# Where the low part of each weight comes from: a subtraction on VectorE, or an accumulating transfer onto the negated rounded block

## The chip, the cores and the metric

The kernel runs on one core of a Trainium2 chip. The metric is device time in microseconds, from one launch of the whole program; the kernel before took 977.54 us as the median of three runs. One core has five engines that take part here: TensorE (PE, matrix products; PEld is its weight load), VectorE (DVE), ScalarE (ACT), GpSimd (POOL) and SyncE (SP, which here only issues transfers). Each engine works through its own queue of instructions in order, and they wait for each other by semaphores. Sixteen DMA engines move data between the chip's memory (HBM) and the on-chip memory (SBUF). Products land in PSUM, from where ScalarE and VectorE fetch them.

## The reference

One inference step of a one-layer hybrid model on 640 tokens (128 context tokens, 512 latent tokens on a grid of 8 x 64), width 1024. With `h` the normed and modulated input:

```python
h = rmsnorm(x, norm1_g) * (1 + sc1) + sh1            # sh, sc, g: six rows from silu(c) @ w_ada
q, k, v, o, gates, u, ga, gb = split(h @ w_in + b_in) # 1024 -> 512*4 + 16 + 1024 + 1024 + 1024
A = (sigmoid(o) * headnorm(mlstm_both_ways(q, k, v, gates))) @ w_proj_a
B = silu(layernorm(dwconv31(glu(u)))) @ w_proj_b
x = x + g1 * ((sigmoid(ga) * A + sigmoid(gb) * B) @ w_out)
h2 = rmsnorm(x, norm2_g) * (1 + sc2) + sh2
gate, val = split(h2 @ w_up)                          # 1024 -> 2 * 2816
x = x + g2 * ((gelu(dwconv3x3(gate)) * val) @ w_down) # 2816 -> 1024
y = rmsnorm(x, final_norm_g)
```

All of it is in float32. The context's final mLSTM states are outputs as well.

## The kernel before

**Products.** Features lie on the 128 partitions, tokens along the free dimension. TensorE works on float32r operands, a rounded form of float32, so every operand is split into a rounded high part and a low part that holds the rest. One 128 x 128 weight block times 128 features then takes three products: high by high, high weight by low input, low weight by high input (`three`, line 443). `mtile` (457) does this for all 640 tokens in two halves of 320, six products for each weight block. `mhalf` (1203) does it for one part of the tokens only, three products for each block. The half-width stages are the output projection (`woA`, `woB`, line 1294), the first columns of the up projection (`upA`, `upB`, 1397), and the second half of the down projection (`dnA` with 384 tokens, `dnB` with 256, line 1466).

**Weight stream.** `_blocks` (82) lists the 1160 weight blocks in the order of their use, eight to a group, 145 groups of 128 x 1024 float32 (512 KB). Three functions feed them:
- `load` (401) has SP load a group from HBM into a staging tile `wst`, of which there are three (NST).
- `prep` (408) splits a group: ScalarE copies `wst` to the rounded `wh`, and VectorE subtracts, `wl = wst - wh`. There are three tiles of `wh` and three of `wl` (NWT), so the tiles of group g + 3 take the place of those of group g.
- `W` (428) hands TensorE its block. On the first block of group g it calls `prep` for g, g + 1 and g + 2 and `load` for g + 3 and g + 4. HELD changes that where two groups are in use side by side: at the start, and in the two v stages (groups 9 and 10, 19 and 20), where no further split is made until both groups are done.

**Order.** The order of all instructions is written out by a planner. `_Order` (143) keeps an estimated clock for every engine; `issue` (203) moves it with each instruction. The main line is the large products. Side lines are generators (norms, gates, the mLSTM scans, the splits of `prep`), which go on when the planner thinks that their operands are there. Background work (convolution taps, the modulation products `ada_tile`, the taps of the feed-forward's convolution) fills VectorE where the planner sees it idle. Every instruction goes through the wrapper `_Timed`, so the profile gives the same line, L139, for all of them, and groups have to be told apart by tile names: `wst`, `wh`, `wl` are the weight stream; `hh`, `hl` the normed input; `h2h`, `h2l` the second one; `mgh`, `mgl` the merged branches; `ah`, `al`, `acth`, `actl` the activations of the feed-forward; `adst` and `ad` the modulation weights; `mm` and `ps` are in PSUM.

**GpSimd** does only memsets, of tiles for the gates (`keep`, `bc`, `dd`, `M`, in `gates`, 792), for the convolution's padding, and of `gbuf` for the feed-forward.

**Start.** x (16 transfers of x in all, eight here) and the first modulation weights (`adst`, 16 transfers of 512 KB) come in while the first products run: for each of the eight feature tiles, four column tiles (`FIRST`) take their products as soon as this tile of the normed input is there. Groups 0 to 3 belong to this stage.

Of the kernel before, what the change touches and what calls it, by code (L numbers as in the profile page):

```python
# [9 lines left out]
F32 = mybir.dt.float32  # L10
# [42 lines left out]
# f tiles in the order of the up projection, and which of them each half of the down projection sums  # L53
# [19 lines left out]
# column tiles whose products run while x and the first modulation come in, then the order of all tiles  # L73
# [8 lines left out]
def _blocks():  # L82
    """Order in which the 128 x 128 weight blocks are used: (matrix, k block, column block)."""
    b = []
    held = {0: 2, 1: 3}
    for k in range(KD):
        b += [(nm, k, m) for nm, m in FIRST]
    for nm, m in ORDER:
        if nm == "v":
            held[len(b) // GB] = len(b) // GB + NWT  # L90
            held[len(b) // GB + 1] = 0
            b += [("v", k, 2 * m + i) for k in range(KD) for i in range(2)]
        else:
            for mm in (m, m + 4) if nm == "u" else (m,):
                if (nm, mm) not in FIRST:
                    b += [(nm, k, mm) for k in range(KD)]
    for nm, m in BRANCH:
        if nm == "g":
            b += [(n, k, m) for n in ("ga", "gb") for k in range(KD)]
        else:  # L100
            b += [("p" + nm, k, m) for k in range(4)]
    b += [("woA", k, m) for m in range(2) for k in range(KD - 1)] + [("woA", KD - 1, m) for m in range(2)]
    b += [("woA", k, m) for m in range(2, 8) for k in range(KD)]
    b += [("woB", k, m) for m in range(8) for k in range(KD)]
    for nm in ("upA", "upB"):
        b += [(nm, k, m) for k in range(KD) for m in (0, NF)] + [(nm, k, 1) for k in range(KD)]
    b += [("up", k, NF + 1) for k in range(KD)]
    for i, (fs, ks) in enumerate(zip(UPS, DNS)):
        for f in fs[2:] if i == 0 else fs:
            b += [("up", k, f) for k in range(KD)]  # L110
            b += [("up", k, NF + f) for k in range(KD)]
        for nm, npre in (("dn", 0),) if i == 0 else (("dnA", 3), ("dnB", 0)):
            b += [(nm, f, m) for m in range(npre) for f in ks[:-1]]
            b += [(nm, ks[-1], m) for m in range(npre)]
            b += [(nm, f, m) for m in range(npre, 8) for f in ks]
    return b, held
# [8 lines left out]
class _Timed:  # L125
    """An engine whose instructions also move an estimate of when their results are there."""
# [17 lines left out]
class _Order:  # L144
    """Emits the instructions of several lines of work in one order: the main line (large products) sets the
    pace, side lines go on when what they last asked of other engines should be there, and background work
    fills VectorE where it would be idle."""
# [55 lines left out]
    def issue(self, key, name, ops, args, kw):  # L203
        out, ins = ops[0], ops[1:]
        acc = kw.get("accum_out")
        t = max([self.free.get(key, 0.0)] + [self.ready.get(a.tensor.name, 0.0) for a in ins if a is not acc])
        if key == "Q":
            t = max(t, self.now)
        t = max(t, self.avail.pop(out.tensor.name, 0.0))
        if key in ("V", "S", "G"):  # L210
            t = max(t, self.ready.get(out.tensor.name, 0.0) - self.LAT)
        t += self.cost(key, name, ops, args, kw) * (2 if key == "PE" and t < COLD else 1)
        self.free[key] = t
        done = t + (2000.0 if key == "Q" else self.LAT)
        for a in (out,) if acc is None else (out, acc):
            self.ready[a.tensor.name] = done
        for a in ops:
            self.used[a.tensor.name] = max(done, self.used.get(a.tensor.name, 0.0))
        if self.line is not None and key in ("V", "S", "G"):
            self.line[0] = max(self.line[0], done)  # L220

    def ring(self, key, tile_, bufs):
        """A tile that takes the place of the one handed out `bufs` tiles before it."""
        names = self.rings.setdefault(key, [])
        names.append(tile_.tensor.name)
        if len(names) > bufs:
            self.avail[names[-1]] = self.used.get(names[-1 - bufs], 0.0)
        return tile_

    def force(self, t):  # L230
        """Runs a side line to its end without regard to the clock."""
        while not t[2]:
            self._go(t)

    def before(self, ops):
        """Background work for the time VectorE would wait for these operands."""
        while self.idle_work() and not self.filling:
            t = max(self.ready.get(a.tensor.name, 0.0) for a in ops[1:] or ops)
            if t < self.free.get("V", 0.0) + HOLE:
                break  # L240
            self.fill()
# [18 lines left out]
    def until(self, *tiles):  # L260
        """Holds a side line until these tiles should be there."""
# [6 lines left out]
    def room(self, key):  # L268
        """Holds a side line while an engine has more than a little left to do."""
# [27 lines left out]
    def fill(self):  # L297
        """One piece of background work, from the lanes in turn: two in a row rarely wait for each other."""
# [19 lines left out]
def tile_trunk(  # L318
# [18 lines left out]
    V, S, G, PE, Q = (_Timed(e, od, k) for e, k in ((nc.vector, "V"), (nc.scalar, "S"), (nc.gpsimd, "G"),  # L337
                                                    (nc.tensor, "PE"), (nc.sync, "Q")))
# [69 lines left out]
    def prep(g):  # L408
        """Splits the eight blocks of group g into two float32r parts that add up to them exactly."""
# [7 lines left out]
        def parts():  # L417
            yield from od.until(src)
            S.activation(hi, src, AF.Copy)
            yield  # L420
            V.tensor_sub(lo, src, hi.bitcast(F32))
# [21 lines left out]
    def three(out, whl, xhl, first, last, shared=0):  # L443
        """out += (hi + lo of one operand) x (hi + lo of the other), without lo x lo. Where two products share the
        bank of their first output, they are one group: one opens it (shared = 1), the other closes it (2)."""
# [18 lines left out]
    def views(pt, t, rows=slice(0, P)):  # L464
        """Where a product lies in PSUM, and the part of a feature-major tile it belongs to."""
# [4 lines left out]
    def split(src, name, hi=None, lo=None):  # L470
        """float32 tile [P, T] -> its two float32r parts."""
# [29 lines left out]
    def rstd(src, w, scale, name):  # L501
        """(src * scale + EPS) ** -0.5, the table's square root refined by one Newton step."""
# [11 lines left out]
    def sqrt_table():  # L514
        """Has the square root's table loaded ahead of its use."""
# [62 lines left out]
    def ada1():  # L578
        """Shift and scale of the first norm, 128 features at a time, and the normed input they give."""
# [190 lines left out]
    def v_tile(p):  # L770
        """v by tokens, heads 2p and 2p + 1."""
# [129 lines left out]
    def setup(p):  # L901
        """Products q k, k by tokens, decay matrices and scaled q of heads 2p, 2p + 1."""
# [295 lines left out]
    def pieces(s):  # L1198
        """Context and latent tokens of a range: (condition, first, end)."""
# [21 lines left out]
    def norm_add(m, s, pc):  # L1221
        """Square of a range of x2[m] now, its column sums once TensorE has other work in between."""
# [4 lines left out]
    def norm_flush():  # L1227
        """Column sums of the squares that should be there."""
# [156 lines left out]
    def dn(fn, mat, m, fs, *args, **kw):  # L1385
        """Down products over f tiles, each taken when it is there."""
# [42 lines left out]
    def square_sum(m, s, sums):  # L1429
        """Adds the square of a range of x2[m] to the sum over the first tiles; the last stays by itself."""  # L1430
# [50 lines left out]
def _columns(v):  # L1481
    """(n * 128,) or (..., n * 128) -> [128, ... n]"""
# [128 lines left out]
```

## Time and profile before

| | before |
|---|---|
| time, median of three runs | 977.54 us (975.96 to 978.05) |
| profiled execution: span, first to last instruction | 976.2 us |
| TensorE busy | 952.3 us, 6796 products |
| VectorE busy | 730.5 us, 1336 instructions |
| ScalarE busy | 362.2 us, 658 instructions |
| GpSimd busy | 6.0 us, 41 instructions |
| moved by DMA | 113.01 MB |
| granted TensorE clock, mean | 0.994 |

The profiled execution has no other time shown than its span; the median of the runs lies 1.3 us above it.

How to read the lines: a line of a group gives line, engine, operation, output tile <- input tiles, shape, count, then busy time and mean ns of one, then the idle time of the engine before them and what ended it. A line of the chain of waits or of the timeline gives the start in us from the span's start, the duration, the engine and the operation. PEld is the weight load of TensorE. A line of a table by stretches gives, after the stretch and its length, the busy time of each engine with its count, then the granted clock, the share of time that the DMA engines were busy, and GB/s. A matmul's duration contains its way through the array; products follow each other about 146 ns apart, though each is shown with some 309 ns.

### The profile page before, as it was taken

What the parts mean: (1) busy time and instruction counts of PE and PEld (TensorE: products, weight loads), DVE (VectorE), ACT (ScalarE), POOL (GpSimd) and SP (SyncE); (2) the same over time, 40 slices, a digit from 0 to 9 for tenths busy, and PEclk for the clock granted to TensorE, in tenths of its full rate; (3) what the DMA queues carried; (4) which work ended last, traced back from release to release, by engine and by line L of the source; (5) the groups of instructions that cost most, each with busy time, mean ns of one, the idle gap of its engine ahead of it and who ended that gap; (6) DMA issues with size and microseconds to landing.
All of it is one profiled execution on the core that took longest, in us unless ns stands there. A gap on an engine that the chain in (4) does not pass through costs nothing.

```text
span 976.2 us, 16639 instructions
## 1 busy us (share of the span) xinstructions
PE 952.3 (98%) x6796; PEld 927.1 (95%) x6796; DVE 730.5 (75%) x1336; ACT 362.2 (37%) x658; POOL 6.0 (1%) x41
## 2 busy tenths in 40 slices
PE   5999999999999999999999999999999999999996
PEld 2799999999998999999999999999999999999995
DVE  3849989998887989898778877985323777675565
ACT  5453434345643422223675333232111232323342
POOL 0100000000000000000000000000000000000000
PEclk9999999999999999999999999999999999999998
DMA  9635122211242355667433222322222222223353
GB/s 355 238 108 87 44 73 66 69 45 55 84 134 76 108 194 183 206 222 274 138 123 117 72 92 76 130 86 66 83 70 65 87 69 84 65 87 95 122 172 109
DMA packets 38971, 113.01 MB, mean 116 GB/s; under 512 B 4336, under 2 KB 7280, under 8 KB 38896
## 3 DMA queue, kind: packets, MB, share of 16 engines
q1 hardware_dynamic: 38896, 111.96, 35.1%
q8 instruction: 53, 0.87, 0.3%
q14 instruction: 22, 0.18, 0.1%
HBM read 108.79 MB, written 3.15 MB: 115 GB/s over the span
## 4 chain that ended last, share of the span: by engine, by line
PE 95%; ACT 2%; DVE 1%; DMA 1%; issue 0%; SPq 0%; DVEq 0%; ACTq 0%
PE mm L139 87%; PE ps L139 8%; DMA x<-in_xT 1%; ACT wh L139 0%; ACT L139 0%; DVE rsy L139 0%; ACT h L139 0%; DVE yo L139 0%; ACT h2h L139 0%; DVE rst L139 0%; ACT sq L139 0%; SPq L139 0%; DVE wl L139 0%; ACT rsy L139 0%; ACT hh L139 0%
## 5 line engine op out<-in xcount | busy, mean ns | idle before, releaser
L139 ACT ACTIVATE wh<-wst 128x1024 fp32r<-128x1024 f32 x145 | 152.9, 1057 | 195.8 <-PE mm L139 175.4
L139 DVE TENSOR_TENSOR wl<-wst,wh 128x1024 fp32r<-128x1024 f32 x145 | 176.3, 1220 | 60.3 <-ACT wh L139 60.1
L139 PE MATMUL mm<-h2h,wh 128*128 128x320 f32 x704 | 164.4, 309 | 0.7 <-ACT h2h L139 0.7
L139 PE MATMUL mm<-h2l,wh 128*128 128x320 f32 x704 | 164.6, 309 | 0.4 <-DVE h2l L139 0.4
L139 PE MATMUL mm<-h2h,wl 128*128 128x320 f32 x704 | 164.0, 308 | 0.0
L139 PE MATMUL mm<-hh,wh 128*128 128x320 f32 (+2 forms) x576 | 134.6, 313 | 3.5 <-ACT wh L139 2.5
L139 PE MATMUL mm<-hl,wh 128*128 128x320 f32 (+2 forms) x576 | 133.4, 311 | 0.0
L139 PE MATMUL mm<-hh,wl 128*128 128x320 f32 (+2 forms) x576 | 133.4, 310 | 0.0
L139 DVE SCALAR_TENSOR_TENSOR acc<-gbuf,cols,acc 128x455 f32<-128x455 f32 (+2 forms) x176 | 129.7, 742 | 4.4
L139 PEld LDWEIGHTS mm<-h2l,wh 128*128 128x128 f32 x704 | 118.8, 188 | 1.1 <-DVE h2l L139 0.9
L139 PEld LDWEIGHTS mm<-h2h,wh 128*128 128x128 f32 x704 | 118.6, 188 | 1.3 <-ACT h2h L139 1.2
L139 PEld LDWEIGHTS mm<-h2h,wl 128*128 128x128 f32 x704 | 118.5, 188 | 0.0
L139 DVE SCALAR_TENSOR_TENSOR z<-glu,cols,z 128x641 f32<-128x641 f32 (+14 forms) x120 | 102.2, 888 | 0.8
L139 PEld LDWEIGHTS mm<-hh,wh 128*128 128x128 f32 x576 | 96.2, 188 | 5.8 <-ACT wh L139 3.0
L139 PEld LDWEIGHTS mm<-hl,wh 128*128 128x128 f32 x576 | 96.4, 188 | 2.1 <-issue 1.3
L139 PEld LDWEIGHTS mm<-hh,wl 128*128 128x128 f32 x576 | 96.8, 188 | 0.7 <-issue 0.7
L139 PE MATMUL mm<-ah,wl 128*128 128x320 f32 (+2 forms) x320 | 85.5, 308 | 0.0
L139 PE MATMUL mm<-ah,wh 128*128 128x320 f32 (+2 forms) x320 | 85.5, 308 | 0.0
L139 PE MATMUL mm<-al,wh 128*128 128x320 f32 (+2 forms) x320 | 85.5, 307 | 0.0
L139 DVE SCALAR_TENSOR_TENSOR junk<-ad,cb 128x512 bf16<-128x512 f32 x128 | 81.9, 686 | 0.0
L139 PEld LDWEIGHTS mm<-ah,wl 128*128 128x128 f32 x320 | 56.7, 188 | 0.1
L139 PEld LDWEIGHTS mm<-al,wh 128*128 128x128 f32 x320 | 56.8, 188 | 0.0
(224 smaller groups left out, 1288.7 us busy)
## 6 DMA issues: line engine op xcount, KB each, us to landing
wst<-in_w SPq DMA_DIRECT2D x145, 512.0 KB, 3.6
ad<-in_ada SPq DMA_DIRECT2D x64, 256.0 KB, 3.0
adst<-in_ada SPq DMA_DIRECT2D x16, 512.0 KB, 10.3
x<-in_xT SPq DMA_DIRECT2D x16, 320.0 KB, 5.7
out_yT<-x SPq DMA_DIRECT2D x8, 192.0 KB, 4.5
cb<-in_crow SPq DMA_DIRECT2D x4, 256.0 KB, 5.6
out_yT<-yo SPq DMA_DIRECT2D x4, 256.0 KB, 2.2
Ca<-in_cst SPq DMA_DIRECT2D x1, 516.0 KB, 6.9
```

The costliest lines, as they stand in the source:

```text
L139: return fn(*args, **kw)
```

## The change

The split of a group no longer has a subtraction. ScalarE writes the rounded copy `wh` as before, and then a second copy of `wst`, scaled by -1, into `wl`: the negated rounded block. Then GpSimd's queue issues a transfer of the same 512 KB from HBM with an accumulate, `wl += w`, which leaves `w - wh` in `wl`. Each weight group is thus read twice from HBM, once by SP into `wst` and once by the accumulating transfer. The planner gets a key "R" for this queue: a transfer starts no earlier than TensorE's estimated clock and the readiness of its output, and its result is there 2000 ns after its modelled cost.

The split's side line now issues its three instructions in one go; before, it gave way to others between the copy and the subtraction. The comments and docstrings of the file are gone too, which changes line numbers only.

```diff
@@ class _Order, issue
-        if key == "Q":
+        if key in ("Q", "R"):
             t = max(t, self.now)
+        if key == "R":
+            t = max(t, self.ready.get(out.tensor.name, 0.0))
...
-        done = t + (2000.0 if key == "Q" else self.LAT)
+        done = t + (2000.0 if key in ("Q", "R") else self.LAT)
@@ tile_trunk
-    V, S, G, PE, Q = (_Timed(e, od, k) for e, k in ((nc.vector, "V"), (nc.scalar, "S"), (nc.gpsimd, "G"),
-                                                    (nc.tensor, "PE"), (nc.sync, "Q")))
+    V, S, G, PE, Q, GQ = (_Timed(e, od, k) for e, k in ((nc.vector, "V"), (nc.scalar, "S"), (nc.gpsimd, "G"),
+                                                        (nc.tensor, "PE"), (nc.sync, "Q"), (nc.gpsimd, "R")))
@@ prep
         def parts():
             yield from od.until(src)
             S.activation(hi, src, AF.Copy)
-            yield
-            V.tensor_sub(lo, src, hi.bitcast(F32))
+            S.activation(lo, src, AF.Copy, scale=-1.0)
+            GQ.dma_start(lo, w_d[g], accum_op=ALU.add)
+            yield
```

## The prediction

> **What bounds the kernel now.** I read the page's busy shares and its chain of waits first, then who TensorE waits for, then single stretches of the timeline.
>
> ```profile
> span 976.2 us, 16639 instructions
> PE 952.3 (98%) x6796; PEld 927.1 (95%) x6796; DVE 730.5 (75%) x1336; ACT 362.2 (37%) x658; POOL 6.0 (1%) x41
> ...
> PE 95%; ACT 2%; DVE 1%; DMA 1%; issue 0%; SPq 0%; DVEq 0%; ACTq 0%
> ```
>
> ```profile
> PE ps L139 <- DVE rsy L139: 3.0, 3, 2.0
> PE mm L139 <- ACT wh L139: 2.5, 1, 2.5
> PE mm L139 <- DVE ga L139: 1.0, 1, 1.0
> ```
>
> TensorE (PE) is busy for 98% of the span and is 95% of the chain. The waits in which it waits for VectorE (DVE) come to about 4 us in all; none names the tile wl that the removed subtraction writes. So lightening VectorE can win some 4 us at best, and the question is whether the new way makes wl late.
>
> ```profile
> L139 ACT ACTIVATE wh<-wst 128x1024 fp32r<-128x1024 f32 x145 | 152.9, 1057 | 195.8 <-PE mm L139 175.4
> L139 DVE TENSOR_TENSOR wl<-wst,wh 128x1024 fp32r<-128x1024 f32 x145 | 176.3, 1220 | 60.3 <-ACT wh L139 60.1
> ...
> wst<-in_w SPq DMA_DIRECT2D x145, 512.0 KB, 3.6
> ...
> adst<-in_ada SPq DMA_DIRECT2D x16, 512.0 KB, 10.3
> ```
>
> ```profile
> q1 hardware_dynamic: 38896, 111.96, 35.1%
> ```
>
> Of the 195.8 us that ScalarE (ACT) idles before wh, 175.4 us end with TensorE. That is the three-buffer ring: wh and wl of group g+2 take the place of those of g-1, so a split can begin only when TensorE has left g-1, and has two group periods until it is used. The timeline of an output projection group shows the margin:
>
> ```profile
> 479.33 0.42 PE L139 MATMUL mm<-mgh,wh 128*128 128x320 f32 x1
> ...
> 480.13 1.05 ACT L139 ACTIVATE wh<-wst 128x1024 fp32r<-128x1024 f32 x1
> ...
> 481.20 1.23 DVE L139 TENSOR_TENSOR wl<-wst,wh 128x1024 fp32r<-128x1024 f32 x1 [1.09 <-ACT wh L139]
> ...
> 483.33 0.41 PE L139 MATMUL mm<-mgh,wh 128*128 128x320 f32 x1
> ...
> 487.31 0.42 PE L139 MATMUL mm<-mgh,wh 128*128 128x320 f32 x1
> ...
> 487.57 0.19 PEld L139 LDWEIGHTS mm<-mgh,wl 128*128 128x128 f32 x1
> ```
>
> Groups start at 479.33, 483.33 and 487.31: a period p of 3.99 us. The split starts 0.80 us after the group's start, wl is there at 482.43, and its first weight load is 0.26 us into the group two later, at 487.57: 5.1 us to spare.
>
> **The change part by part.** *Removed:* 145 subtractions, 145 x 1.220 = 176.9 us of VectorE. As TensorE hardly waits for VectorE, I take 0; bounds are 0 and the 4 us above. VectorE's background taps then run earlier, which TensorE does not wait for either.
>
> *Added on ScalarE:* 145 negated copies of the same shape as wh: 145 x 1.057 = 153 us, to 53% of the span. Each holds back evacuations of PSUM behind it by 1.06 us, covered by the second product buffer for one period. Where ScalarE itself is on the chain there is no cover:
>
> ```profile
> 503.87 1.06 ACT wh L139
> ...
> 509.04 1.04 ACT wh L139
> ...
> 512.09 1.05 ACT wh L139
> 513.14 0.02 issue
> 513.16 1.23 DVE wl L139
> ```
>
> Three copies are added there and one subtraction leaves: 3 x 1.05 - 1.23 = +1.9 us. With late weights in these six groups as well I take +4; bounds 2 and 15.
>
> *Added on DMA:* 145 accumulating transfers of 512 KB, issued from GpSimd's queue. The load by SP stays, so in_w is read twice, and each transfer also reads wl back. Let L be the time from the end of the negated copy to landing. No row shows an accumulate or a transfer issued by GpSimd. From below: 3.6 us, the plain load of the same bytes, of which this does everything and more. From above: 10.3 us, the same size in the crowded start. Between: queue q1 took 0.351 x 976.2 / 111.96 = 3.06 us per MB, 1.6 us for 0.524 MB; reading wl back should cost that again, 3.6 + 1.6 = 5.2, and about 1 us for descriptors in software, for which no row stands (0 to the 5.1 us left below 10.3). I take L = 6.2 where DMA is quiet and 7.8, one load of 1.6 us more, where it is crowded; nearer to 3.6 than to 10.3, since most of the program is not like the start.
>
> The Trainium skill (Collectives: The Full Stack, section "The bandwidth ceiling") says that an add in the DMA path costs not for the arithmetic but for its second source read, which halved the rate there (1.93). By that the accumulate's data would take twice a load's 1.6 us, as assumed; no trace here shows it yet.
>
> The allowed L follows from the timeline. From group start to the end of hi and negated copy: 0.80 + 2 x 1.06 + about 0.1 of semaphore = 3.02; use at 2p + 0.26. So **L must be under 2p - 2.8**, and beyond it each group costs (L - 2p + 2.8) / 2. Periods, by stage:
>
> ```profile
> 514.85 417.94 PE mm L139 x2795
> ```
>
> ```profile
> 894.62 1.06 ACT L139 ACTIVATE wh<-wst 128x1024 fp32r<-128x1024 f32 x1 [2.50 <-PE mm L139]
> 898.81 1.06 ACT L139 ACTIVATE wh<-wst 128x1024 fp32r<-128x1024 f32 x1 [3.13 <-PE mm L139]
> ```
>
> ```profile
> 0.00:40.00 40.00, 28.97 (x256) 17.74 (x257) 18.46 (x52) 19.33 (x34) 4.26 (x33) 0.96 0.91 352
> 441.00:465.00 24.00, 24.00 (x201) 22.00 (x199) 19.75 (x50) 9.71 (x14) 0.00 (x0) 1.00 0.71 250
> 465.00:503.00 38.00, 38.00 (x310) 35.66 (x310) 25.96 (x46) 24.42 (x44) 1.30 (x2) 1.00 0.41 134
> ...
> 934.80:964.90 30.10, 30.10 (x275) 29.80 (x274) 21.66 (x36) 12.76 (x18) 0.00 (x0) 1.00 0.49 158
> ```
>
> (After the busy times come granted clock, DMA share and GB/s.) A full group is 48 products of 149.5 ns, p = 7.2, so L may be 11.6: **no cost** for some 97 of 145 groups. The half-width groups pay:
> - Output projection, 16 groups, p = 3.99, allowed 5.2. Five are in the stretch with DMA at 0.71: (7.8 - 5.2) / 2 x 5 = 6.5; eleven at (6.2 - 5.2) / 2 = 5.5. Sum 12.
> - First part of the last down projection (384 tokens), 11 groups, p = 4.2 (894.62 to 898.81), allowed 5.6: 0.3 x 11 = 3.3.
> - Second part (256 tokens), 11 groups in 30.1 us, p = 2.74, allowed 2.7. **This is below even the plain load's 3.6.** With loads, accumulates and outputs together it is crowded: (7.8 - 2.7) / 2 x 11 = 28.
> - The two v stages hold two groups at once, so the next group is split one period ahead: allowed 7.2 - 2.8 = 4.4, (6.2 - 4.4) x 2 = 3.6.
> - The start:
>
> ```profile
> 22.17 1.04 ACT L139 ACTIVATE wh<-wst 128x1024 fp32r<-128x1024 f32 x1
> ...
> 23.63 1.22 DVE L139 TENSOR_TENSOR wl<-wst,wh 128x1024 fp32r<-128x1024 f32 x1
> ...
> 26.99 0.36 PEld L139 LDWEIGHTS mm<-hh,wl 128*128 128x128 f32 x2
> ```
>
> The copies end at about 24.3, wl is wanted at 26.99, and DMA is 0.91 busy: 24.3 + 7.8 - 27.0 = 5.1.
>
> *Queue of GpSimd.* Each transfer waits there for its negated copy; behind it stand the memsets and later transfers. The gate memsets now come after the first groups' transfers:
>
> ```profile
> 25.15 1.91 POOL L139 MEMSET keep<- 64x640 f32 x11 [8.73 <-PE ps L139]
> ```
>
> They would run some tens of us later, and with the gate scans held back; TensorE has the q, k and u tiles to do meanwhile, so 0, and about 4 us (these and three of 0.63) without that cover. SP's loads gain a little: a wst buffer comes free after the copy instead of the later subtraction.
>
> **Sum:** 5.1 + 3.6 + 12 + 4 + 3.3 + 28 = 56, so 976.2 + 56 = 1032 of span. The median of the runs (977.54) is 1.3 above this span, whose own execution has no other time shown: **1033 us.** With L = 3.6 everywhere: 0.9 + 0 + 0 + 2 + 0 + 5 = 8, or 985. With 10.3 everywhere: 7.6 + 11.8 + 41 + 15 + 26 + 42 = 143, or 1121.
>
> **Rivals.** *Not slower: VectorE's relief.* If the transfers land as fast as the subtraction did, within 2.7 us in the 256-token part, nothing stalls, and the waits on rsy and ga (4.0 us) plus the subtraction on the chain at 513.16 (1.2) go: 977.5 - 5 = 972. It speaks for it that 97 groups have 11.6 us; against it that the plain load alone takes 3.6, and that the 4 us are mostly reciprocals and not queueing. It decides at L = 2.7. If it lands at about 3, losses and gains meet: no change, 977.
>
> *Saturated DMA.* If an accumulate occupies the 16 engines for four times a load (6.4 us), group and load need 8.0 us against a period of 7.2, and the full groups bind too: 145 x 8.0 = 1160, plus the 37 MB of other transfers, partly under it: about 1200. It decides at 7.2 - 1.6 = 5.6 us per accumulate. For it: elementwise work in the DMA path is nowhere in this trace. Against: the share is 35%, and would be 35 + 145 x 3.2 / 976 = 83% by my estimate.
>
> *The clock falls with the stalls.* If gaps of 1 to 2.5 us in every half-width group lower the granted clock to half, their products take twice as long: output projection +64, second down part +30, against the 40 they cost by stalls: 1033 + 54 = 1087. Against it: in the first 40 us TensorE is idle for 11 us and the clock is 0.96. The Trainium skill (TensorE: Matmul & The Clock Gate, section "HAM oscillation") says that idle gaps beyond about 3.4 us put the clock back to half; by that rule gaps of my size would be too short, and the row of the start agrees as far as it goes.
>
> *Not what it says:* the subtraction is gone from the program text, and exactly one copy and one transfer stand in its place; I give this nothing.
>
> **How the numbers follow.** Late weights in the half-width stages, as summed: 0.70, own range 985 to 1080. Saturated DMA 0.12, clock 0.05, relief 0.06, no change 0.07. This kernel's measurement can tell about 0.2% (2 us) from no change. So faster 0.06, same 0.07, slower 0.87. The range takes in the bounds of L (985 to 1121), part of the no-change case below and part of the saturated case above: 978 to 1145.
>
> **What would show it.** wl should be written by ScalarE 145 times at 1.06 us and by a GpSimd transfer, with DMA at about 188 MB; VectorE near 554 us, ScalarE near 515. TensorE should wait for the DMA of wl in the output projection, from about 935 on and near 27 us, and not in full-width stretches. Median issue-to-landing of the accumulate should be 5 to 8 us. The forecast is wrong if that is under 4 us, or above 11, or if TensorE's new waits name something else than wl.

## The result and the profile after

The changed kernel takes 1080.51 us (median of four runs, 1079.84 to 1082.76) against 976.75 us of the kernel before (four runs, the three above among them): a ratio of 1.107, 95% interval 1.105 to 1.109, 104 us slower. The prediction of 1033 us had the direction, most of the places, and 56 of the 104 us. The time lies inside its range of 978 to 1145, at the upper edge of the 985 to 1080 that it gave to late weights by themselves.

The page of the kernel after, its busy shares, queues and issues (an issue line ends with the median us from issue to landing):

```profile
span 1078.1 us, 16901 instructions
...
PE 983.9 (91%) x6795; PEld 952.0 (88%) x6796; DVE 572.1 (53%) x1191; ACT 496.5 (46%) x803; POOL 131.9 (12%) x186
...
q0 software_dynamic: 20880, 76.03, 38.5%
q1 hardware_dynamic: 38896, 111.96, 33.4%
...
wst<-in_w SPq DMA_DIRECT2D x145, 512.0 KB, 4.1
wl<-in_w POOLq DMA_DIRECT2D x145, 512.0 KB, 7.6
ad<-in_ada SPq DMA_DIRECT2D x64, 256.0 KB, 5.6
```

Three things are to be seen. VectorE lost 158 us of work, as meant, and that bought nothing. The accumulate lands after 7.6 us, where a plain load took 3.6 before, and the other loads became slower beside it (wst 3.6 to 4.1, ad 3.0 to 5.6; the line of ad in the kernel before is the one below). And TensorE, with the same number of products, was idle for 94.2 us instead of 23.9, but was also *busy* for 31.6 us longer.

```profile
ad<-in_ada SPq DMA_DIRECT2D x64, 256.0 KB, 3.0
```

Whom TensorE's products wait for, longest first:

```profile
PE mm L139 <- DMA wl<-in_w: 62.1, 27, 6.0
PE ps L139 <- ACT sq L139: 8.4, 5, 4.3
PE mm L139 <- DVE ga L139: 8.2, 1, 8.2
```

The first row is new: 27 waits of up to 6.0 us for the low part. The third was 1.0 us. One of the 27, in the timeline of the output projection:

```profile
498.50 0.19 PEld L139 LDWEIGHTS mm<-mgh,wh 128*128 128x128 f32 x1
...
499.28 1.04 ACT L139 ACTIVATE wh<-wst 128x1024 fp32r<-128x1024 f32 x1
...
500.23 1.04 ACT L139 ACTIVATE wl<-wst 128x1024 fp32r<-128x1024 f32 x1
...
501.56 0.86 POOL L139 DMA_DIRECT2D wl<-in_w  x1 [10.53 <-ACT wl L139]
...
506.47 0.19 PEld L139 LDWEIGHTS mm<-mgh,wh 128*128 128x128 f32 x1
...
507.39 1.04 ACT L139 ACTIVATE wh<-wst 128x1024 fp32r<-128x1024 f32 x1
...
509.06 0.19 PEld L139 LDWEIGHTS mm<-mgh,wl 128*128 128x128 f32 x1 [2.29 <-DMA wl<-in_w]
```

A group starts at 498.50, the copies begin 0.78 us later and end at 501.27. The group two later starts at 506.47 and would want its low part at about 506.7; it comes at 509.06, 7.8 us after the copies. The copies for a later group begin at 507.39, while TensorE waits: they need the group before this one to be over, and not its low part.

Cut at the last product of the start and at the first products with the convolution's output, the merged branches and the feed-forward's activations, so that a stage holds the same products in both kernels, the table by stretches reads as follows (busy time and count of each engine, then granted clock, DMA share, GB/s), first for the kernel before, then for the kernel after:

```profile
0.00:63.10 63.10, 52.07 (x424) 40.07 (x424) 33.38 (x80) 28.80 (x48) 4.26 (x33) 0.97 0.73 271
63.10:334.00 270.90, 268.46 (x1963) 262.10 (x1962) 238.34 (x475) 123.99 (x277) 0.44 (x6) 1.00 0.26 73
334.00:432.10 98.10, 98.10 (x673) 98.10 (x672) 87.74 (x208) 23.87 (x28) 0.00 (x0) 1.00 0.55 182
432.10:495.00 62.90, 62.90 (x503) 59.02 (x502) 48.33 (x100) 32.93 (x54) 1.30 (x2) 1.00 0.62 213
495.00:668.60 173.60, 172.53 (x1182) 170.96 (x1182) 145.08 (x224) 66.08 (x121) 0.00 (x0) 1.00 0.29 96
668.60:886.10 217.50, 217.50 (x1485) 217.50 (x1485) 125.47 (x166) 55.39 (x90) 0.00 (x0) 1.00 0.24 76
886.10:965.00 78.90, 78.90 (x562) 77.86 (x561) 47.24 (x74) 30.43 (x40) 0.00 (x0) 1.00 0.42 134
```

```profile
0.00:77.20 77.20, 56.65 (x423) 43.85 (x424) 26.91 (x74) 34.37 (x54) 9.24 (x36) 0.89 0.81 262
77.20:365.40 288.20, 271.77 (x1962) 265.95 (x1962) 231.89 (x532) 153.60 (x309) 28.81 (x41) 0.98 0.61 144
365.40:478.60 113.20, 103.16 (x671) 102.37 (x671) 69.69 (x186) 35.83 (x41) 11.25 (x13) 0.96 0.82 233
478.60:564.30 85.70, 70.59 (x504) 64.04 (x502) 19.12 (x48) 48.34 (x71) 13.60 (x17) 0.92 0.85 192
564.30:746.00 181.70, 175.60 (x1181) 173.84 (x1181) 105.36 (x154) 90.63 (x147) 24.86 (x30) 0.98 0.72 161
746.00:963.40 217.40, 217.40 (x1486) 217.40 (x1485) 90.63 (x134) 83.74 (x121) 26.84 (x31) 1.00 0.69 150
963.40:1067.00 103.60, 87.07 (x562) 83.26 (x560) 23.65 (x53) 49.28 (x60) 17.30 (x20) 0.93 0.88 207
```

The two side by side, in us, with the prediction's terms:

| stage | before | after | longer | of it TensorE idle | of it busy | predicted |
|---|---|---|---|---|---|---|
| start | 63.1 | 77.2 | 14.1 | 9.5 | 4.6 | 5.1 |
| first tiles, mLSTM, first gates | 270.9 | 288.2 | 17.3 | 14.0 | 3.3 | 3.6 |
| branch gates and projections | 98.1 | 113.2 | 15.1 | 10.0 | 5.1 | 0 |
| output projection (half width) | 62.9 | 85.7 | 22.8 | 15.1 | 7.7 | 12 |
| first up columns (half width) and first up stretch | 173.6 | 181.7 | 8.1 | 5.0 | 3.1 | 4 |
| full-width down and second up stretch | 217.5 | 217.4 | -0.1 | 0 | -0.1 | 0 |
| last down projection (half width) | 78.9 | 103.6 | 24.7 | 16.5 | 8.2 | 31 |
| sum | | | 102 | 70 | 32 | 56 |

The longer busy time goes with the granted clock. Two neighbouring stretches of the output projection, and two neighbouring products out of each:

```profile
490.50:497.30 6.80, 4.83 (x18) 4.83 (x19) 0.00 (x0) 0.00 (x0) 0.53 (x1) 0.50 1.01 244
497.30:504.10 6.80, 6.80 (x65) 6.18 (x64) 1.35 (x4) 3.43 (x5) 0.86 (x1) 1.00 0.30 61
```

```profile
493.17 0.47 PE L139 MATMUL mm<-mgl,wh 128*128 128x320 f32 x1
493.44 0.47 PE L139 MATMUL mm<-mgh,wl 128*128 128x320 f32 x1
...
499.05 0.31 PE L139 MATMUL mm<-mgh,wh 128*128 128x320 f32 x1
499.19 0.31 PE L139 MATMUL mm<-mgl,wh 128*128 128x320 f32 x1
```

At clock 0.50 the products follow each other 0.27 us apart, at 1.00 0.147 us. The mean clock fell from 0.994 to 0.963: between one spell at half clock near 23 us and one at the very end, which both kernels have, the trace's clock record of the kernel after has 14 more, of 3.4 or 6.8 us each, and that of the kernel before has none. In all spells but the last one TensorE was busy for 59.2 us (3.4 before). At the two spacings that makes about 25 of the 31.6 us, an estimate; what makes the other 7 is not shown.

### The profile page after: what moved, and what is told of

Its sections match the earlier page's. It is cut to its first block, busy times and chain, and to the rows that moved or that the text cites. A ratio compares the mean times of both kernels' runs of the same rounds, so it can differ in the third digit from the quotient of the medians.

```text
span 1078.1 us, 16901 instructions
## 1 busy us (share of the span) xinstructions
PE 983.9 (91%) x6795; PEld 952.0 (88%) x6796; DVE 572.1 (53%) x1191; ACT 496.5 (46%) x803; POOL 131.9 (12%) x186
## 3 DMA queue, kind: packets, MB, share of 16 engines
q0 software_dynamic: 20880, 76.03, 38.5%
## 4 chain that ended last, share of the span: by engine, by line
PE 58%; issue 23%; DMA 12%; POOL 3%; DVE 2%; ACT 1%; SPq 0%; POOLq 0%; DVEq 0%; ACTq 0%
PE mm L139 53%; DMA wl<-in_w 8%; PE ps L139 5%; DMA ad<-in_ada 3%; POOL wl L139 2%; DVE junk L139 1%; DMA cb<-in_crow 1%; DMA x<-in_xT 1%; ACT wh L139 0%; DVE z L139 0%; DVE yo L139 0%; SPq L139 0%; DVE rsy L139 0%; ACT wl L139 0%; ACT sq L139 0%
## 5 line engine op out<-in xcount | busy, mean ns | idle before, releaser
L139 POOL DMA_DIRECT2D wl<-in_w x145 | 126.1, 870 | 926.1 <-ACT wl L139 739.9
L139 PE MATMUL mm<-h2h,wl 128*128 128x320 f32 x704 | 166.3, 312 | 6.1 <-DMA wl<-in_w 6.1
L139 ACT ACTIVATE wl<-wst 128x1024 fp32r<-128x1024 f32 x145 | 151.8, 1047 | 0.0
L139 PE MATMUL mm<-hh,wl 128*128 128x320 f32 (+2 forms) x576 | 136.3, 316 | 13.4 <-DMA wl<-in_w 13.4
L139 PE MATMUL mm<-ah,wl 128*128 128x320 f32 (+2 forms) x320 | 88.9, 319 | 16.5 <-DMA wl<-in_w 16.3
L139 PEld LDWEIGHTS mm<-hh,wh 128*128 128x128 f32 x576 | 98.6, 192 | 5.5 <-ACT wh L139 3.0
L139 DVE SCALAR_TENSOR_TENSOR x<-mm,mods,x 128x128 f32<-128x128 f32 (+3 forms) x48 | 18.7, 434 | 125.3 <-PE mm L139 125.3
```

Of the source, the lines that this page charges most:

```text
L139: return fn(*args, **kw)
```

## The experiments

The theory at this point: the accumulate lands too late for groups that are used in short time; the waits bring the clock down; and the extra traffic delays other loads. The rivals: ScalarE's extra copies or the changed order of VectorE's work; a price on total traffic wherever it runs; the software queue and not the accumulate.

### No transfer at all

```diff
             S.activation(lo, src, AF.Copy, scale=-1.0)
-            GQ.dma_start(lo, w_d[g], accum_op=ALU.add)
+            od.issue("R", "dma_start", [lo, w_d[g]], (), {})
```

> The kernel after without its 145 accumulating transfers: the order of all instructions, the planner's estimate for the transfer and ScalarE's negated copy stay, so wl holds the negated block and not the low part. If the loss of about 104 us comes from the transfers (late landing, shared DMA engines, and the clock that follows), this takes 974 to 982 us and TensorE's granted clock is back at 0.99. If ScalarE's extra 152 us of copies, or the new order of VectorE's background work, carry a good part of it, it stays above 1000 us.

979.03 us, ratio 1.0024 (1.0009 to 1.0040). ScalarE was busy for 496.1 us and VectorE for 572.8, as in the kernel after, and the clock was 0.994. So 2.4 us of the 104 belong to copies and order, and the rest needs the transfers. VectorE's relief, net of the copies that ScalarE gets for it, is worth nothing even with no transfer to pay for it.

### A plain transfer in place of the accumulate

```diff
-            GQ.dma_start(lo, w_d[g], accum_op=ALU.add)
+            GQ.dma_start(lo, w_d[g])
```

> The same transfers from GpSimd's queue, at the same places and after the same waits, but plain: they overwrite wl with the weights, so the low part is not computed. If the second read of an accumulate is what is dear, landing falls from the 7.6 us median by 1.3 us or more (to 5.5 to 6.3), the share of the DMA engines of this queue falls from 38.5% to about 23%, and the time to between 1020 and 1050 us. If the software queue itself is what is dear, landing stays above 7 us and the time above 1065 us.

1014.70 us, ratio 1.040 (1.038 to 1.042). Time and landing (4.7 us) both lie below what was expected, on the side of the second read. The queue and the issues of this run:

```profile
q0 software_dynamic: 20880, 76.03, 21.3%
...
wst<-in_w SPq DMA_DIRECT2D x145, 512.0 KB, 3.7
wl<-in_w POOLq DMA_DIRECT2D x145, 512.0 KB, 4.7
```

A plain transfer by GpSimd lands 1.0 us after one by SP of the same size. The accumulate adds 2.9 us to that. In engine time it is 0.385 x 1078.1 / 76.03 = 5.46 us per MB against 0.213 x 1012.4 / 76.03 = 2.84, a factor of 1.92. So the accumulate is the larger part, 66 of the 102 us beyond the run without transfers, and a plain second read costs the other 36. That the landing grows by 2.9 us while the engine time for 0.524 MB grows by only 1.4 is not explained by these runs; GpSimd's issue itself takes 865 ns for an accumulate and 527 ns for a plain transfer, 0.3 us of it at most.

### Only the half-width groups, only the full-width groups

```diff
             S.activation(hi, src, AF.Copy)
-            S.activation(lo, src, AF.Copy, scale=-1.0)
-            GQ.dma_start(lo, w_d[g], accum_op=ALU.add)
-            yield
+            if 49 <= g < 71 or g >= 123:      # the other run: 73 <= g < 123
+                S.activation(lo, src, AF.Copy, scale=-1.0)
+                GQ.dma_start(lo, w_d[g], accum_op=ALU.add)
+                yield
+            else:
+                yield
+                V.tensor_sub(lo, src, hi.bitcast(F32))
```

> Accumulating transfers only for groups 49 to 70 (output projection, first up columns) and 123 to 144 (last down projection); subtraction on VectorE for all others. If the loss is local to the stage whose groups come late, these stages lose what they lost in the kernel after, 22.7 + 8.2 + 24.7 = 56 us, and the time is 1025 to 1040 us. If the loss grows with the total of extra traffic, 44 of 145 groups give about 104 x 44 / 145 = 32 us, 1005 to 1012 us.

1040.43 us, ratio 1.067 (1.065 to 1.069): 64 us for 44 groups, a little above the local forecast and twice the price by traffic. Some 5 of the 8 us beyond 56 have a visible place, the output projection, which took 91 us instead of 85.7. With the subtractions still on VectorE, the modulation loads reach into this stage, where 14 of them landed after a median of 10.1 us; that these loads are the cause was not tested in this kernel.

> Accumulating transfers only for groups 73 to 122, the full-width up and down products of the feed-forward, where a group has some 11 us; subtraction elsewhere. If a transfer that lands inside its margin costs nothing, the time is within 2 us of the kernel before (975 to 979 us), though 50 of 145 subtractions are gone from VectorE. If the extra traffic costs everywhere, about 104 x 50 / 145 = 36 us are lost, 1010 us; if VectorE's relief is worth something, it is up to 4 us faster than before.

976.85 us in 12 runs, ratio 1.0004 (0.9993 to 1.0015). 50 accumulates that land after 7.5 us inside a margin of some 11 cost nothing, and 50 subtractions less (with 50 copies more on ScalarE) win nothing. The stretch in question:

```profile
665.30:882.80 217.50, 217.50 (x1485) 217.50 (x1484) 91.75 (x135) 81.86 (x119) 25.02 (x29) 1.00 0.67 147
```

217.5 us, as before; VectorE at 91.75 us instead of 125.5. The price on total traffic is out.

### Only the start

The same switch with `g < 9`.

> Accumulating transfers only for groups 0 to 8 (the start and the first full-width tiles), subtraction for the rest. If the start's 14 us are its own late weights (wl of the first groups landing behind the crowded loads of x and the modulation, and the half clock that follows the gaps), the time is 986 to 993 us. If they come from the changed order of the whole program, which the run without transfers put at 2.4 us, it is 976 to 980 us.

992.76 us, ratio 1.017 (1.015 to 1.019), 17 us for nine groups. Of the span, 12.2 us of this are in the start (75.3 us). The median landing of these transfers was 8.9 us, and two waits for wl made 11.1 us.

### The modulation's loads taken away

```diff
         if n < 64:
             t, i = divmod(n, 2)
-            st = adp2.tile([P, 512], F32, tag="ad", name="ad")
-            Q.dma_start(st, ada2_d[t, :, 512 * i:512 * i + 512])
-            adq[n] = st
+            if n < NAD:
+                st = adp2.tile([P, 512], F32, tag="ad", name="ad")
+                Q.dma_start(st, ada2_d[t, :, 512 * i:512 * i + 512])
+                held_ad.append(st)
+            adq[n] = held_ad[n % NAD]
```

> The kernel after with only the first four of the 64 loads of the second modulation weights (256 KB each); the modulation products then read these four tiles again and again, so 60 tiles of it are left out and the modulations are not the reference's. If the 25 to 30 us lost between 309 and 478 us come from accumulates and these loads crowding each other, with VectorE's in-order queue waiting for the loads and ScalarE's copies for VectorE, this stretch goes back to within 8 us of its 148 us of before and the time falls to 1048 to 1062 us. If the stretch is slow because its own wl lands late, the time stays above 1070 us.

1052.69 us, ratio 1.077 (1.073 to 1.082), 28 us below the kernel after. In the kernel after, the longest waits of all engines between 330 and 478 us are these:

```profile
POOL wl L139 <- ACT wl L139: 135.4, 17, 21.5
ACT mgh L139 <- DVE ga L139: 70.7, 7, 19.7
DVE junk L139 <- DMA ad<-in_ada: 34.8, 20, 5.0
```

This is a chain through queues. The modulation products (junk) wait for loads that have become slow; the branch's sums (ga) stand behind them on VectorE; ScalarE's rounding (mgh) waits for ga, up to 19.7 us; and behind mgh on ScalarE stand the copies of later weight groups, and behind these the accumulates. In the whole kernel before, mgh never waited for ga longer than 7.0 us. One link of the chain in the timeline:

```profile
452.86 0.74 ACT L139 ACTIVATE mgh<-ga 128x640 fp32r<-128x640 f32 x1 [19.70 <-DVE ga L139]
453.51 1.04 ACT L139 ACTIVATE wh<-wst 128x1024 fp32r<-128x1024 f32 x1
...
463.23 0.90 PE L139 MATMUL mm<-hAh,wl 128*128 128x320 f32 x2 [5.09 <-DMA wl<-in_w]
```

The copies of this group end at 455.50, and the accumulate lands 7.7 us later, no later than elsewhere; it is the copies that come late. Without the loads, the same stages read:

```profile
75.50:358.20 282.70, 271.48 (x1964) 265.39 (x1963) 230.79 (x531) 153.42 (x309) 27.96 (x40) 0.99 0.56 125
358.20:456.50 98.30, 98.30 (x673) 98.30 (x672) 69.61 (x188) 36.25 (x42) 12.11 (x14) 1.00 0.70 161
```

The branches' stage is back at 98.3 us (98.1 before), with the accumulates still in it, so its 15.1 us needed both, accumulates and loads. The stage ahead of it keeps 11.8 of its 17.3 us; three waits for wl make 6.5 us of this, and longer busy time 3.0.

### A ring of four

```diff
-NA = 38
+NA = 37
-NST = 3
-NWT = 3
+NST = 2
+NWT = 4
```

> The kernel after with four buffers of wh and wl in place of three, so a split can begin three group periods ahead; for room there are two staging tiles in place of three and 37 general tiles in place of 38. If the landing time alone sets the loss in the half-width groups, the allowed landing becomes 3p - 2.8 (9.2 us in the output projection, 9.8 and 5.4 in the two parts of the last down projection) and only the last part loses, about 10 us: 1005 to 1020 us. If the DMA engines' throughput sets it there (1.7 us for a load plus 2.9 for an accumulate, 4.6 us per group against periods of 3.99, 4.2 and 2.74), those stages still lose about 10 + 4 + 20 us and the time is 1025 to 1045 us. If the start and the branches, which a deeper ring should help little, carry the loss, it stays above 1055 us.

> The control for the ring of four: the kernel after with two staging tiles and 37 general tiles, and still three buffers of wh and wl. All theories expect about the time of the kernel after, 1075 to 1095 us; what it differs by is the price of the smaller pools.

1055.88 us, ratio 1.081 (1.079 to 1.083); the control 1091.40 us, ratio 1.118 (1.114 to 1.121), so the smaller pools alone cost 11 us. The fourth buffer gives back 36 us of that, and the third forecast holds, if narrowly: the start and the branches keep most of their loss. In the run with the ring of four TensorE waited 28.6 us for ga, in the control 14.5. Output projection and last down projection, ring of four, then control:

```profile
473.50:549.40 75.90, 66.05 (x508) 60.52 (x510) 19.41 (x48) 45.60 (x66) 13.00 (x15) 0.96 0.92 217
947.00:1039.50 92.50, 83.79 (x562) 81.27 (x560) 23.47 (x53) 47.33 (x58) 16.43 (x19) 0.96 0.94 226
```

```profile
481.00:567.40 86.40, 70.52 (x508) 63.33 (x510) 19.06 (x48) 49.01 (x71) 14.35 (x18) 0.94 0.86 202
964.60:1077.50 112.90, 87.61 (x558) 84.05 (x560) 23.43 (x52) 49.12 (x60) 17.29 (x20) 0.91 0.84 195
```

75.9 and 92.5 us against 86.4 and 112.9: half of what was lost there (62.9 and 78.9 before). A DMA share of 0.92 and 0.94 speaks for the engines' throughput as what remains, so that a still deeper ring would not help; no run tested that.

### What a gap costs by itself

The kernel before, with gaps of known length ahead of the ten gate tiles of the second up stretch; in the other run, ahead of the gate and the value tiles with two copies in place of six:

```diff
+    def gap():
+        a = ps()
+        PE.matmul(a[:, 0:TH], lhsT=h2[0][0][:, 0:P], rhs=h2[0][0][:, 0:TH], start=True, stop=True)
+        t = sm.tile([P, T], F32R, tag="gap", name="gap", bufs=1)
+        for s in HALF:
+            S.activation(t[:, s], a[:, 0:TH], AF.Copy)
+        for _ in range(6):
+            S.activation(t, t.bitcast(F32), AF.Copy)
+        b = ps()
+        PE.matmul(b[:, 0:TH], lhsT=t[:, 0:P], rhs=t[:, 0:TH], start=True, stop=True)
```

> The kernel before with ten added gaps of about 5 us each on TensorE (a chain of eight copies on ScalarE that starts from a product of TensorE and that its next product waits for), one ahead of each gate tile of the second up stretch. If one gap beyond some 3.4 us sets the clock to half for one or two windows, each gap costs its own 5 us and 1.7 to 3.4 us of slower products: 976 + 50 + 17 to 34 = 1043 to 1060 us, with about ten spells of half clock. If the clock goes by the share of idle time over a longer stretch, it stays near 0.99 and the time is 1022 to 1032 us, as with the short gaps.

> The kernel before with twenty added gaps of about 2.4 us each (four copies), ahead of each gate and each value tile of the same stretch: about the same idle time, 48 us, in shorter pieces. If only long gaps set the clock to half, it stays at 0.99 and the time is 976 + 48 = 1020 to 1030 us. If idle time as such does, it loses about as much clock as the long gaps, 1040 us and more.

1058.11 us (ratio 1.082, 1.080 to 1.084) and 1053.55 us (1.078, 1.076 to 1.080). The waits of TensorE and the mean clock, long gaps and then short gaps:

```profile
PE ps L139 <- ACT gap L139: 54.7, 10, 5.5
```

```profile
core 0: 1057.8 us, clock 0.960
```

```profile
PE ps L139 <- ACT gap L139: 54.1, 20, 3.0
```

```profile
core 0: 1050.6 us, clock 0.983
```

The gaps came out at 5.5 us, and at 2.45 and 3.0 us in turn, the idle time equal at 54 us. Beyond it the long gaps cost 978.7 - 952.3 = 26.4 us of longer busy time, the short ones 973.0 - 952.3 = 20.7, in which the 20 and 40 added products have their part. With every one of the ten long gaps the trace's clock record shows a spell of 6.8 us at half clock. The short ones brought a spell of 3.4 us in 7 of 20 cases: 4 of the ten of 3.0 us, 3 of the ten of 2.45 us. TensorE was busy for 46.9 us in the spells of the long gaps and for 23.9 us in those of the short ones; at 0.27 and 0.147 us per product that is 21 and 11 us of slower products, an estimate. So neither expectation held whole: at equal idle time longer gaps cost about twice the clock, but no length down to 2.45 us was safe. In the kernel after, two waits of 1.7 and 1.9 us (ended at 523.87 and 540.37) each had a spell of 3.4 us just behind them.

No run here points to a version that beats the kernel before: the best use of the change, in the full-width groups alone, is level with it.

## Why the prediction was right, and where it was off

**What bounds the kernel: right.** TensorE set the time, and taking up to 158 us from VectorE was worth 0 net of ScalarE's copies, with the transfers (full-width groups only) and without them. The rival of relief falls. The memsets that stand behind the transfers in GpSimd's queue, put at 0, show in no wait of TensorE.

**The margin of two periods: right in kind.** The new waits name wl, the start, the output projection and the last down projection lost most, and the full-width feed-forward lost nothing. The stalled group above follows the step of the prediction line by line.

**The price of a late group: put at a half, nearer a third.** The prediction divides the lateness, L - 2p + 2.8, by two. But the copies at 507.39 began inside the stall that ended at 509.06, so a stall does not hold back the next split. It delays only the start of the group behind it, and the split that begins there is wanted two groups on: one stall in three groups. So it was in the second half of the output projection, where stalls ended at 523.87, 540.37 and 556.92 and three splits began between each two of them. By estimate, with the stage's landing (8.0 us, 8.3 from the end of the copies), a third of the lateness gives (8.3 - 5.2) / 3 x 16 = 16.5 us and a half gives 25; TensorE idled for 15.1. The 12 us predicted came near by luck: the landing was put too short and the price too high. In the last down projection a third is still too much (27 us with a landing of 7.9, against 16.5 idle), which stays open.

**The landing time: under-sized where DMA is quiet.** Quiet was put at 6.2 us from the end of the copies and measured 7.5 from the issue (full-width groups only), which begins 0.3 us after the copies; crowded was put at 7.8, and measured 8.0 to 8.9 from the issue in the output projection, the branches and the start, but 7.6 in the last down projection. The 1 us for the software queue was right (4.7 against 3.7); the accumulate's own part was put at 1.6 and is 2.9. The rule of the Trainium skill (Collectives: The Full Stack, section "The bandwidth ceiling"), that an add costs by its second source read, agrees with the engine time here: 1.92 against 1.93 there.

**"No cost for some 97 groups": the step that failed first.** It held for the 50 of the feed-forward and not for the other 45, groups 4 to 48, whose two stages lost 32 us together against 3.6 for the v stages. In the branches it failed for a reason that the margin doesn't contain: the other loads became slow, and three in-order queues passed the delay on. The prediction counted the queue of GpSimd and the share of DMA time, but not who else waits for transfers on SP's queue. Its sign that TensorE would not wait in full-width stretches failed here, with three waits for wl of 10.0 us in all. Without those loads the branches lost nothing. Of the stage ahead some 11 us are left beyond what order and loads explain; three late wl make 6.5 of them, and why they were late is open.

**The clock: the second.** The prediction set half clock beside the stalls as a rival of 0.05 and said that gaps of 1 to 2.5 us would be too short. It is no rival but an addend: of the 102 us of span, 70 are idle and 32 longer busy time, some 25 of it at half clock. The waits were up to 6.0 us, not 2.5, since they bunch (27 waits, and not one in every group), and the added gaps show that even 2.45 us can do it. The rival's own time, 1087, lies nearer to the measured one than 1033, but its reason does not hold: it put all products of the output projection and of the last down projection's second part at half clock, and there were 14 spells in the whole program. The Trainium skill (TensorE: Matmul & The Clock Gate, section "HAM oscillation") puts the limit at gaps of about 3.4 us; the spells of 3.4 and 6.8 us here agree with its window, but as a limit for gaps the measurement stands against it.

**Two terms that erred the other way.** The last down projection was put at 31 us of stalls and had 16.5 of idle time, and with the clock 24.7. The start was put at 5.1 and lost 14.1, 9.5 of it idle: its transfers landed at 8.9 and not 7.8, and for two groups.

**Saturated DMA: not as a whole.** An accumulate occupies the engines 1.9 times as long as a plain transfer, not four times, and the full-width groups did not bind; but in the last down projection the share was 0.88, and in the ring of four 0.94, where throughput may have bound.

## What to carry to other kernels

Where one engine is busy for 98% and waits for a second one for 4 us, work taken from the second is worth nothing, and everything that goes in its place on a longer path is measured against the shortest margin on the way, not the mean one. Before adding transfers, list who else waits for transfers at that time and what stands behind these waiters in their in-order queues. And count a stall of TensorE of a few us as more than its length: here longer busy time, most of it slower products after the gaps, added nearly half of the idle time again (32 to 70 us).

## What the runs showed of the hardware

- An accumulating transfer of 512 KB from HBM into SBUF landed after 7.5 us in quiet stretches, a plain one by GpSimd after 4.7, one by SP after 3.7; in engine time the accumulate took 5.46 us per MB and the plain one 2.84.
- GpSimd was occupied for 865 ns by each issue of an accumulate, and for 527 ns by a plain one.
- TensorE went to half clock with gaps of 5.5 us in 10 of 10 cases, of 3.0 us in 4 of 10, and of 2.45 us in 3 of 10; its 320-column products then followed each other 0.27 us apart instead of 0.147.
